# Turning one more head's output rows by transfers, between the steps of the last head's softmax

## The chip, the cores and the metric

The kernel runs on one core of one Trainium2 chip. The metric is the device time of one execution in microseconds (us). The kernel before was run three times: 1340.91, 1341.71 and 1341.49 us, median 1341.49 us.

## The reference

Two layers of a token backbone over 256 context tokens and 256 latent tokens of width 1024. Layer 0 mixes tokens with an mLSTM in two directions, layer 1 with multi-head attention; each is followed by a gated convolutional feed-forward, and a layer norm stands behind every sub-layer. The change lies in layer 0, between the last head's mixing and the output projection:

```python
def out(h_in, s):                                   # s: what the scan gives, per head
    o = jax.nn.sigmoid(h_in @ w_og).reshape(Bq, T, M_HEADS, M_DV)
    hsum = o * s.transpose(0, 2, 1, 3)              # the gate times the mixed values
    return _head_rms_norm(hsum, norm_g) @ w_out     # RMS norm per head, projection
```

There are four heads of 512 columns, 512 tokens (context first), and `w_out` is 2048 x 1024. The chunked scan is written in the kernel as one masked and normalised product per head, called its softmax here: exponentials of gate differences times the scores, a division, and the product with the values.

## The kernel before

Everything runs on one core and TensorE (PE) is busy throughout. A float32 product is made of three matmuls of rounded halves (`mm3`, lines 447, 450, 451): hi x hi, hi x lo, lo x hi. So every operand is written twice: a hi half, which ScalarE (ACT) casts, and a lo half, which VectorE (DVE) subtracts. Weights come through a stream: SyncE (SP) loads `raw` tiles, ACT casts them (line 361, `w` or `wu`), DVE subtracts (line 384).

The head loop in `build` goes over h = 0 to 3. In pass h the projection to queries and keys of head h (`w_qk`) fills PE, and background steps are taken between its weight tiles, by `tick`: the softmax of head h-1 (`head`), and the turn of the output rows of head h-2. Then `av` multiplies head h-1's softmax with its values, and `s_mm` makes head h's scores (tiles `sc`, `sl`, copied to `S` by ACT at line 1065).

*The softmax*, `head`: `aB` rows are loaded, DVE adds a mask (`Am`, line 1078), ACT takes exponentials (line 1115), DVE multiplies with the scores and sums (line 1116), divides (lines 1122 to 1133), and in a later step PE turns the result `W` in twelve 128x128 blocks (`PT`, line 1147), whose halves are cut at lines 461 and 462.

*The output rows*, `post`: `tt` are four tiles `oh` of 128 tokens x 512 columns, the product of `av` times the gate (DVE, line 1207). ACT squares and sums them (line 1217) and takes a root (line 1218), DVE inverts it (line 1219) and scales the rows (line 1221). The projection needs them turned (columns by tokens), as `hn`, four tiles for each head. There are two ways:

- By transfers, for heads 0 and 1: ACT copies the two 16-bit planes of each row tile apart (`pl`, line 466), the POOL queue writes them to DRAM (`hd`, line 1228), and ACT's queue loads them back turned (`hx`, line 1269, four transposes for each head). ACT and DVE make `hn` from `hx` (lines 1277 and 1278). `mixed` interleaves these steps with a softmax by a string of steps, in which `h` is a step of the softmax, `p` one of `post` (planes and writes), `L` a transpose and `S` the two halves of one `hn` tile.
- By PE, for heads 2 and 3: sixteen 128x128 turns into PSUM (`hnT`, line 1236), from which ACT and DVE make `hn` (lines 1243 and 1244).

After the loop comes the projection `mout`: sixteen weight tiles k, four for each head, 12 matmuls each for the first group of 256 tokens (`y`). Tiles 0 to 7 need heads 0 and 1. Between them run two background steps a tile: first all of head 3's softmax, then head 2's `post`. Also between them, head 3's values and gate rows are loaded (`v_steps`). Then `av(3)`, `post(3)` between tiles 8 to 11, and tiles 12 to 15. A scheduler then orders each engine's instructions; engines work in that order. Background work of another kind, sums for the layers' modulation (line 566, with its `ar` loads on SP and a one-element copy on ACT, line 581), is taken in between.

Of the kernel before, what the change touches and what calls it, by code (L numbers as in the profile page):

```python
# [416 lines left out]
class K:  # L417
# [827 lines left out]
            self.hn[k] = u  # L1245
        yield

    def mixed(self, head, post):

        plan = "p hp h hL h hL . L hS LS h S S . . ."  # L1250
        for step in plan.split():
            for op in step:
                if op in "hp":
                    next(head if op == "h" else post, None)
                elif op == "L":
                    self.turn_load()
                elif op == "S":
                    self.turn_split()
            yield
# [1106 lines left out]
def build(tc, off, a, out):  # L2366
    es = ExitStack()
    with es:
        k = K(tc, es, off, a)
# [14 lines left out]
        S = None  # L2384
        tt = None
        k.hn, k.turned, k.hx = {}, [], []
        for h in range(H0):
            gens = []
            if h == 0:
                gens.append(k.gate_chain())  # L2390
            if h >= 2:
                gens.append(k.mixed(k.head(h - 1, S), post))
            elif h >= 1:
                gens.append(k.head(h - 1, S))
            k.bg = gens
            k.w_qk(h, 2, (lambda: k.v_load(h - 1)) if h >= 1 else None)
            k.drain()
            if h >= 1:
                tt = k.av(h - 1)
                if h < 3:  # L2400
                    post = k.post(h - 1, tt)
                    next(post)
            S = k.s_mm(h)
        k.xc = None
        hn = lambda i: (k.hn[i][:, 0], k.hn[i][:, 1])
        pc = k.acc4()
        k.bg = [k.head(3, S, True), k.post(2, tt, True)]
        vs = k.v_steps(3)
        for i in range(8):
            k.outmm("mout", range(i, i + 1), hn, pc, 0, 16, 2)  # L2410
# [2 lines left out]
        tt = k.av(3)  # L2413
# [135 lines left out]
```

## Time and profile before

| | before |
|---|---|
| median of three runs | 1341.49 us |
| the profiled execution | 1341.12 us |
| its span in the profile | 1339.1 us |
| PE busy | 1326.7 us (99%) |
| DVE busy | 1077.2 us (80%) |
| ACT busy | 729.9 us (55%) |

Rows of a timeline give the start and the length in us, the engine, the line, the operation, the tiles and shapes, and, in brackets, how long the engine had been idle and what released it. Lengths overlap a little where an engine works without a pause, so the distance from one start to the next is what one instruction costs there. A row of waits names who waited for whom, the total, the times and the longest. Head 2's softmax and the way back of head 1 lie at 505 to 559 us of the span, head 3's softmax and the turn of head 2 at 571 to 598, `av(3)` at 598 to 606, and the turn of head 3 at 612.

### The profile page before, as it was taken

The page shows a single profiled execution, that of the slowest core. Times are in us where ns is not written, and L with a number is a line of the kernel's source. Part 1 is how long each engine was busy: PE and PEld are TensorE (multiplying, and loading weights), DVE is VectorE, ACT ScalarE, POOL GpSimd, SP SyncE. Part 2 cuts the span into 40 slices and gives each one's busy share as a digit, 9 for nine tenths or more (in the row PEclk, how much of TensorE's full clock was granted, in tenths as well). Part 3 has the DMA queues.
Part 4 walks back from the last instruction along what each step waited for, and adds up shares of the span by engine and source line. Part 5 has one row for each costly group of instructions (what it writes and reads, how often), then busy time and mean ns, then how long its engine had stood idle before and what let it go on. Part 6 is the DMA issues. An engine that isn't in the chain of part 4 may idle for free.

```text
span 1339.1 us, 18750 instructions
## 1 busy us (share of the span) xinstructions
PE 1326.7 (99%) x6573; PEld 1111.3 (83%) x6573; DVE 1077.2 (80%) x1783; ACT 729.9 (55%) x1271; POOL 165.3 (12%) x268
## 2 busy tenths in 40 slices
PE   8999999999999999999999999999999999999997
PEld 5777888888888888888898888888888988988876
DVE  4798957678688596987979978768899889899996
ACT  4765544445734555574643334333567768567772
POOL 0212000011110111120002011111000022020100
PEclk9999999999999999999999999999999999999999
DMA  9988947889685486875628989967967597497791
GB/s 366 324 276 290 333 161 252 243 270 313 235 262 190 156 245 200 295 276 209 228 75 276 322 264 283 280 177 180 321 223 221 175 243 222 165 303 233 250 336 49
DMA packets 116990, 325.52 MB, mean 243 GB/s; under 512 B 21416, under 2 KB 40360, under 8 KB 116624
## 3 DMA queue, kind: packets, MB, share of 16 engines
q1 hardware_dynamic: 64288, 223.37, 48.6%
q0 software_dynamic: 33360, 81.43, 22.7%
q10 hardware_dynamic: 19248, 19.54, 4.5%
q8 instruction: 51, 0.84, 0.2%
q14 instruction: 43, 0.35, 0.1%
HBM read 289.51 MB, written 56.80 MB: 259 GB/s over the span
## 4 chain that ended last, share of the span: by engine, by line
PE 98%; DVE 1%; DMA 0%; issue 0%; ACT 0%; SPq 0%; DVEq 0%; ACTq 0%
PE fin L1573 8%; PE y L450 6%; PE y L451 6%; PE y L447 6%; PE tok L447 6%; PE tok L450 6%; PE tok L451 6%; PE fin L447 6%; PE fin L451 6%; PE fin L450 6%; PE qk L447 4%; PE qk L451 4%; PE qk L450 4%; PE up L746 2%; PE up L447 2%; PE up L450 1%
## 5 line engine op out<-in xcount | busy, mean ns | idle before, releaser
L361 ACT CAST w<-raw 128x1024 fp32r<-128x1024 f32 (+2 forms) x290 | 300.0, 1037 | 263.6 <-PE tok L451 74.1
L384 DVE TENSOR_TENSOR w<-raw,w 128x1024 fp32r<-128x1024 f32 (+2 forms) x290 | 347.7, 1202 | 114.5 <-ACT w L361 111.0
L566 DVE SCALAR_TENSOR_TENSOR junk<-ar,bc 128x1024 f32<-128x1024 f32 x128 | 155.8, 1218 | 5.1 <-ACT bc L608 2.2
L450 PE MATMUL fin<-h,w 128*128 128x512 f32 (+1 forms) x370 | 139.6, 377 | 0.0
L447 PE MATMUL fin<-h,w 128*128 128x512 f32 (+1 forms) x370 | 139.5, 377 | 0.0
L451 PE MATMUL fin<-h,w 128*128 128x512 f32 (+1 forms) x370 | 139.3, 377 | 0.0
L1573 PE MATMUL fin<-h,w 128*128 128x512 f32 (+1 forms) x636 | 111.1, 337 | 0.0
L1573 PEld LDWEIGHTS fin<-h,w 128*128 128x128 f32 x636 | 97.6, 190 | 13.2
L447 PE MATMUL qk<-xc,w 128*128 128x512 f32 x256 | 100.1, 391 | 0.0
L451 PE MATMUL qk<-xc,w 128*128 128x512 f32 x256 | 99.7, 389 | 0.0
L450 PE MATMUL qk<-xc,w 128*128 128x512 f32 x256 | 99.6, 389 | 0.0
L450 PEld LDWEIGHTS fin<-h,w 128*128 128x128 f32 x370 | 69.6, 188 | 13.0
L451 PEld LDWEIGHTS fin<-h,w 128*128 128x128 f32 x370 | 69.6, 188 | 12.9
L447 PEld LDWEIGHTS fin<-h,w 128*128 128x128 f32 x370 | 69.6, 188 | 12.6
L451 PEld LDWEIGHTS qk<-xc,w 128*128 128x128 f32 x256 | 48.0, 188 | 10.0
L447 PEld LDWEIGHTS qk<-xc,w 128*128 128x128 f32 x256 | 48.1, 188 | 9.9
L450 PEld LDWEIGHTS qk<-xc,w 128*128 128x128 f32 x256 | 48.1, 188 | 9.9
L384 DVE TENSOR_TENSOR wu<-raw,wu 128x1024 fp32r<-128x1024 f32 (+1 forms) x42 | 49.6, 1205 | 4.7 <-ACT wu L361 4.3
L447 PE MATMUL tok<-w,hT 128*128 128x512 f32 x128 | 49.9, 390 | 0.0
L450 PE MATMUL tok<-w,hT 128*128 128x512 f32 x128 | 49.8, 389 | 0.0
L451 PE MATMUL tok<-w,hT 128*128 128x512 f32 x128 | 49.8, 389 | 0.0
L763 ACT ACTIVATE fg<-fg 128x512 f32<-128x512 f32 (+1 forms) x44 | 23.1, 525 | 47.6 <-DVE fg L761 41.2
(520 smaller groups left out, 3146.4 us busy)
## 6 DMA issues: line engine op xcount, KB each, us to landing
raw<-in_ws SPq DMA_DIRECT2D x279, 512.0 KB, 5.3
ar<-in_adaT SPq DMA_DIRECT2D x80, 512.0 KB, 5.7
t4d<-in_ws POOLq DMA_DIRECT2D x20, 512.0 KB, 8.6
zd<-in_ws POOLq DMA_DIRECT2D x18, 512.0 KB, 11.3
adaw<-in_ada SPq DMA_DIRECT2D x16, 512.0 KB, 7.9
raw<-zd SPq DMA_DIRECT2D x12, 512.0 KB, 5.2
zr<-fd ACTq DMA_DIRECT2D x33, 128.0 KB, 4.9
xmd<-xr POOLq DMA_DIRECT2D x16, 256.0 KB, 4.6
```

The source lines that it names most:

```text
L361: self.cast = k.nc.scalar.copy(h[:, :cols], src)
L384: i = self.k.nc.vector.tensor_sub(l[:, :n], src, h[:, :n])
L447: q = mm(out, w[0], x[0], start=start, stop=False, skip_group_check=on)
L450: mm(out, w[0], x[1], start=False, stop=False, skip_group_check=on)
L451: mm(out, w[1], x[0], start=False, stop=stop, skip_group_check=on)
L566: nc.vector.scalar_tensor_tensor(o, w, 1.0, self.bc[j], op0=ALU.mult, op1=ALU.mult, accum_out=col[:, k, j:j + 1])
L746: nc.tensor.matmul(ps[m], wk[i][:, c], hT[k][:, j], start=made[m] == 0, stop=made[m] == 23)
L763: nc.scalar.activation(tmp[:, :n], tmp[:, :n], AF.Silu)
L1573: self.nc.tensor.matmul(ps[:, 0:256] if x else ps, w[x][:, k * 128:(k + 1) * 128], h[:, 0:256] if x else h, start=i == 0 and not k0, stop= ...
```

## The change

Head 2's rows go by transfers too. `post` of head 2 is begun where head 2's product is made, ahead of head 3's scores, as for heads 0 and 1; so its squares, root and scaling stand there. `mixed` gets its string as an argument, and for the last softmax takes its ten steps first but for `post`'s planes and writes after the fourth, then the four transposes and the four pairs of halves:

```diff
-    def mixed(self, head, post):
-
-        plan = "p hp h hL h hL . L hS LS h S S . . ."
+    def mixed(self, head, post, plan="p hp h hL h hL . L hS LS h S S . . ."):
...
                 tt = k.av(h - 1)
-                if h < 3:
-                    post = k.post(h - 1, tt)
-                    next(post)
+                post = k.post(h - 1, tt)
+                next(post)
             S = k.s_mm(h)
...
-        k.bg = [k.head(3, S, True), k.post(2, tt, True)]
+        k.bg = [k.mixed(k.head(3, S, True), post, "h h h h p h h h h h h LL L L S S S S")]
```

Lines behind `mixed` move up by one. The built order changes on all engines between head 2's product and head 3's turn, and nowhere else. The string's `L` come behind `PT` there. Three places follow, first before, then after.

PE, the turns of head 3's softmax. `W` without a number is the tile of blocks 0 and 1 and that of block 3; `W_5091` and `W_5103` are the same tile, block 2:

```order
L447 MATMUL y<-wu,hn 128x512
L1147 MATMUL PT<-ident,W 128x128 x2
L1147 MATMUL PT<-ident,W_5091 128x128 x2
L1147 MATMUL PT<-ident,W 128x128 x2
L1147 MATMUL PT<-ident,W_5091 128x128 x2
L450 MATMUL y<-wu,hn 128x512
```

```order
L451 MATMUL y<-wu,hn 128x512
L1147 MATMUL PT<-ident,W 128x128 x6
L1147 MATMUL PT<-ident,W_5103 128x128 x2
L1147 MATMUL PT<-ident,W 128x128 x2
L1147 MATMUL PT<-ident,W_5103 128x128 x2
L447 MATMUL y<-wu,hn 128x512
```

Before, the four turns of blocks 0 and 1 stood 16 matmuls ahead of these eight, 24 behind the first `y<-wu`; now all twelve stand together, 36 behind it. The sixteen `hnT` of head 2, which stood 15 matmuls behind the eight, are gone.

ACT, from the last squares of head 2 (before) and the planes (after) to the next weight cast:

```order
L1217 ACTIVATE jk,ss<-oh 128x512 x2
L1218 ACT_TABLE_LOAD
L1218 ACTIVATE ss<-ss,keps 128x4
L461 CAST PT<-PT 128x512 x2
L1243 ACTIVATE hn<-hnT,sm 128x512 x4
L361 CAST w<-raw 128x1024
```

```order
L466 COPY pl<-oh 128x1024 x4
L461 CAST v<-vr 128x512
L361 CAST w<-raw 128x1024
L461 CAST v<-vr 128x512
L461 CAST PT<-PT 128x512 x3
L1268 DMA_TRANSPOSE hx<-hd 128x1024 x4
L1276 ACTIVATE hn<-hx,sm 128x512 x4
L361 CAST w<-raw 128x1024
```

The squares and the root of head 2, with a table load, now stand ahead of head 3's exponentials, which get a table load of their own; the root of head 3 gets a third.

DVE, from head 2's lo halves to the scaling of head 3's rows:

```order
L1244 SCALAR_TENSOR_TENSOR hn<-hnT,sm,hn 128x512 x4
L384 TENSOR_TENSOR w<-raw,w 128x1024
L1207 TENSOR_TENSOR oh<-av,oh 128x512 x2
L566 SCALAR_TENSOR_TENSOR junk,mod_84<-ar,bc 128x1024
L1207 TENSOR_TENSOR oh<-av,oh 128x512 x2
L1219 RECIPROCAL ss<-ss 128x4
L1221 TENSOR_SCALAR oh<-oh,ss 128x512 x4
```

```order
L1277 SCALAR_TENSOR_TENSOR hn<-hx,sm,hn 128x512 x4
L1207 TENSOR_TENSOR oh<-av,oh 128x512 x2
L384 TENSOR_TENSOR w<-raw,w 128x1024
L1207 TENSOR_TENSOR oh<-av,oh 128x512
L566 SCALAR_TENSOR_TENSOR junk,mod_84<-ar,bc 128x1024 x2
L1207 TENSOR_TENSOR oh<-av,oh 128x512
L1219 RECIPROCAL ss<-ss 128x4
L1221 TENSOR_SCALAR oh<-oh,ss 128x512 x4
```

The lo halves stand at the same place but read `hx`; one more sum (line 566) stands ahead of the last of head 3's products with the gate. Head 2's own inverse and scaling moved ahead of head 3's mask. On the POOL queue the four writes of `hd` stand ahead of the four gate loads `oh` of head 3.

## The prediction

> **What bounds the kernel now.** I read the page first, then who PE waited for, then the chain and the three engines' timelines around the change. The page's head, PE's row and the chain by engine:
>
> ```profile
> span 1339.1 us, 18750 instructions
> PE 1326.7 (99%) x6573; PEld 1111.3 (83%) x6573; DVE 1077.2 (80%) x1783; ACT 729.9 (55%) x1271; POOL 165.3 (12%) x268
> PE 98%; DVE 1%; DMA 0%; issue 0%; ACT 0%; SPq 0%; DVEq 0%; ACTq 0%
> ```
>
> PE is the bound from end to end. Its waits over the span (us in total, times, longest) are five rows, of which the largest and the smallest stand here; each came once, and none lies near the change:
>
> ```profile
> PE idle L683 <- DVE adav L519: 1.5, 1, 1.5
> ...
> PE up L746 <- DVE hT L721: 0.3, 1, 0.3
> ```
>
> So an instruction taken from PE is worth its whole time, if PE then finds everything else ready. The profiled execution took 1341.12 us, 2.0 us of it outside its span; the median is 1341.49. I add changes to the median: 0.4 us, within the spread of the three runs (1340.91 to 1341.71). About 0.2% (2.7 us) is what a measurement of this kernel can tell from no change.
>
> **What goes.** The chain in order of time, start and length, at the turns of head 2's softmax (543), of head 3's (587, 591) and of head 2's output rows (595):
>
> ```profile
> 543.40 1.31 PE PT L1147 x12
> ...
> 587.00 0.44 PE PT L1147 x4
> ...
> 591.11 0.87 PE PT L1147 x8
> ...
> 595.41 1.75 PE hnT L1236 x16
> ```
>
> The 16 turns of head 2 go: **1.75 us** off PE. The twelve PT turns stand in one piece after the change; that saves nothing, since 0.44 + 0.87 = 1.31, as head 2's twelve took. 1.75 us is 0.13%, so even the whole gain is inside what can't be told from none. hn's hi and lo halves are still made for head 2, by ACT and DVE, from hx instead of PSUM.
>
> **First place: does PE wait for the last softmax?** Before, by PE's order shown with the change, only the first four turns (blocks 0 and 1) stood 24 matmuls after the first `y<-wu`, the other eight 16 matmuls later. Now all twelve stand after 36; the fifth is the first that needs the last W. The rows of before that time this, PE and then DVE:
>
> ```profile
> 581.39 0.39 PE L447 MATMUL y<-wu,hn 128*128 128x512 f32 x1
> 598.16 0.39 PE L447 MATMUL av<-v,PT 128*128 128x512 f32 x1
> 606.32 0.39 PE L447 MATMUL y<-w,hn 128*128 128x512 f32 x1
> 611.77 1.91 PE L1236 MATMUL hnT<-ident,oh 128*128 128x128 f32 x16
> ```
>
> ```profile
> 571.32 0.68 DVE L1207 TENSOR_TENSOR oh<-av,oh 128x512 f32<-128x512 f32 x1
> 577.24 1.22 DVE L384 TENSOR_TENSOR w<-raw,w 128x1024 fp32r<-128x1024 f32 x1 [2.90 <-ACT w L361]
> 578.38 0.28 DVE L1116 SCALAR_TENSOR_TENSOR W<-W,S 128x128 f32<-128x128 f32 x1
> 584.42 0.67 DVE L462 TENSOR_TENSOR v<-vr,v 128x512 fp32r<-128x512 f32 x1
> 585.01 0.48 DVE L1131 TENSOR_SCALAR W<-W,R 128x512 f32<-128x512 f32 x1
> 590.01 0.75 DVE L1133 SCALAR_TENSOR_TENSOR W<-W,R 128x512 f32<-128x512 f32 x1
> ```
>
> 36 matmuls take 8.16 us (598.16 to 606.32), so PE reaches the turns at 581.39 + 8.16 = 589.55 and the fifth 0.44 later, at 590.0. DVE: L1219 and L1221 of head 2 (1.8 us) now stand ahead of the softmax of head 3, mostly in the 2.90 us in which DVE waited for ACT. ACT has head 2's root by about 574.9: the last L1207 ends at 572.0, then come a square (0.7), one S (0.6), the table load (1.3) and the root (0.3). Then DVE: 1.8 for L1219 and L1221, one Am (0.6), the `w` split (1.14), the other Am (0.6), to 579.1. Its rows from L1116 to the last L1133 took 578.38 to 590.76, 12.4 us. Behind that L1133 the order now has one `w` split (577.24 to 578.38, 1.14 us) and two `v` splits (584.42 to 585.01, 0.6 each) that stood ahead of it: 10.0 us remain. With 0.9 us of waiting for ACT's exponentials (next part; an estimate) W is ready at 579.1 + 10.0 + 0.9 = 590.0, as PE asks for it. I take 0.1 us of waiting, from 0 to 1.
>
> **What it adds on ACT.** ACT's rows; the first three are from the turn of head 0, whose rows go by transfers already, the rest from the place of the change:
>
> ```profile
> 459.50 3.88 ACT L466 COPY pl<-oh 128x1024 uint16<-128x1024 uint16 x4
> 465.74 1.28 ACT L1115 ACT_TABLE_LOAD   x1
> 467.10 0.40 ACT L1115 ACTIVATE W<-Am,gcol 128x128 f32<-128x128 f32 x1
> ...
> 571.00 0.59 ACT L1065 ACTIVATE S<-sc 128x512 f32<-128x512 f32 x1
> 577.11 0.69 ACT L1115 ACTIVATE W<-Am,gcol 128x128 f32<-128x128 f32 x2
> 582.28 0.60 ACT L461 CAST v<-vr 128x512 fp32r<-128x512 f32 x1
> 582.79 2.00 ACT L361 CAST w<-raw 128x1024 fp32r<-128x1024 f32 x2
> 589.46 1.28 ACT L1218 ACT_TABLE_LOAD   x1
> 590.75 0.30 ACT L1218 ACTIVATE ss<-ss,keps 128x4 f32<-128x4 f32 x1
> ```
>
> Before, one table load (589.46) served the roots of heads 2 and 3. Now head 2's root comes ahead of head 3's exponentials and head 3's behind, so there are three: root, exponential, root, two more. The Trainium skill, "ScalarE: Activation LUTs", section "What ACT_TABLE_LOAD costs", gives about 1283 ns for the load and 1380 ns of drain with it. The trace agrees on the first and shows no drain: 589.46 + 1.28 = 590.74 and L1218 runs at 590.75; with the drain each added load would cost 2.66.
>
> The four squares and head 2's root (about 4 x 0.7 + 1.6 us) fall in ACT's waits before 576 us. Then the second load (465.74 to 467.10: 1.36), one exponential and a late Am (0.5) delay the exponentials from 582.28 to 584.1. A `v` cast (0.5), a `w` cast (1.0) and the four pl copies (3.88) bring ACT to 589.5.
>
> **Second place: the way back.** hx and hd of heads 0 and 1 and the issues around them:
>
> ```profile
> L1269 ACTq DMA_TRANSPOSE hx<-hd x8: 1174/1208/1496, 471.7 to 534.4; - x8
> L1277 ACT ACTIVATE hn<-hx,sm x8: 722/727/746, 489.0 to 553.7; 128x512 fp32r<-128x512 f32 x8
> L1278 DVE SCALAR_TENSOR_TENSOR hn<-hx,sm,hn x8: 742/745/752, 493.0 to 558.9; 128x512 fp32r<-128x512 f32 x8
> DMA to landing us min/median/max: 3.4/3.6/4.4
> ...
> hd<-pl POOLq DMA_DIRECT2D x8, 256.0 KB, 3.1
> ```
>
> The last hd is issued at 589.5 and lands at 592.6; four transposes go out 1.21 apart, the last at 596.2. Their landing is 3.4 to 4.4 us; I take 4.1, since oh, xres and gate load beside them: 600.3. The last hi half (0.73) and lo half (0.75) end at 601.8. The projection asks for head 2's rows only at 606.32 - 1.65 = 604.7, so these halves themselves are on time. On POOL the `oh` loads of head 3 now stand behind hd:
>
> ```profile
> 584.35 1.26 POOL L1188 DMA_DIRECT2D oh<-od  x2 [9.85 <-PE y L450]
> ```
>
> They leave at about 590 instead of 584, some ten us before their use; no cost.
>
> But DVE works in order. By its rows shown with the change, head 3's four L1207 (its product times the gate, from which L1219 and L1221 make the norm that hnT waits for) now stand behind the four lo halves, which wait for a transfer, and a second L566 has slipped in ahead of the last. Their rows before:
>
> ```profile
> 601.78 1.22 DVE L566 SCALAR_TENSOR_TENSOR junk<-ar,bc 128x1024 f32<-128x1024 f32 x1
> ...
> 606.52 0.69 DVE L1207 TENSOR_TENSOR oh<-av,oh 128x512 f32<-128x512 f32 x1 [2.03 <-PE av L451]
> 608.39 0.18 DVE L1219 RECIPROCAL ss<-ss 128x4 f32<-128x4 f32 x1 [1.18 <-ACT ss L1218]
> 608.61 1.67 DVE L1221 TENSOR_SCALAR oh<-oh,ss 128x512 f32<-128x512 f32 x4
> ```
>
> From 601.8: three L1207 (0.6 each), a `w` split (1.1) and two L566 (2.4) put the last L1207 at 607.1. From it to the end of L1221 took 606.52 to 610.28, 3.8 us; the third table load now lies in that path: 607.1 + 3.8 + 1.3 = 612.2. PE can start 0.3 earlier (the third row block is turned first): 611.9. It arrives at 611.77 - 1.75 + 0.1 = 610.1, so it waits **1.8 us**. The same path without a late hx (av ends at 604.7) would end by 609.8: no wait. Ends: 0, and 5.1 if the transposes land as late as other loads do in this stretch (below).
>
> The same engine's later rows (two `w` splits, hnT's lo halves) shift with L1221 and keep about a microsecond before PE's use. SP's next `ar` load waits for the first L566, now some 12 us later; the weights queued behind it run six buffers ahead of their use, 2.7 us each (12 matmuls), so that costs nothing. Outside this stretch the two orders are the same.
>
> **Sum.** -1.75 + 0.1 + 1.8 = +0.15 us on 1341.49: about **1341.6 us**.
>
> **Rivals.**
> 1. *The whole gain.* Transfers are 2 us quicker than I take them, or ACT gets to the pl copies sooner. For: hx at its shortest (3.4) saves 0.7, and ACT's half microsecond waits are my estimates. Against: it needs all of them. 1341.49 - 1.75 = 1339.7.
> 2. *Slower: the transposes land late.* This stretch's xres loads, before the change:
>
> ```profile
> DMA to landing us min/median/max: 5.2/7.4/10.2
> 1.50 3.40 PE L683 MATMUL idle<-zero 128*128 128x512 f32 x8 [1.50 <-DVE adav L519]
> ```
>
> These loads now share the engines with the transposes. Were hx to land as slowly (7.4), 3.3 us more, hnT would wait 5.1: -1.75 + 0.1 + 5.1 = +3.5, 1344.9. An idle PE may also restart slowly: the first eight matmuls took 3.40 us where eight take 1.8 in the stretch above, 1.6 more, 1346.5. (The Trainium skill, "TensorE: Matmul & The Clock Gate", part 1, halves the clock after an idle window of about 3.4 us; no run here has shown so long a wait in mid-kernel.) Against: heads 0 and 1 landed within 4.4 with vr and oh loading beside them. It decides from a wait of 4.4 us at hnT, hx landing near 6.7.
> 3. *A table load holds ACT longer than its row.* Say it takes as long again (1.3), with work queued behind it. The load ahead of the exponentials then delays W and the pl copies by 1.3, and the one ahead of hnT adds 1.3: PE waits 1.4 at PT and 3.1 at hnT. -1.75 + 1.4 + 3.1 = +2.75: 1344.2. L1218's row, 0.01 us behind its load, speaks against it. By the drain that the Trainium skill gives (section above), 1.38 instead of 1.3, it would be 1344.4.
>
> **How the numbers follow.** Forecast (hnT waits 1 to 4 us, 1340.8 to 1343.8): 0.60. Whole gain or nearly (below 1340.8): 0.24. Late transposes: 0.10. Longer table loads: 0.03. Something outside this stretch that gains more than 2.7: 0.03. Range 1339.6 to 1344.4: the whole gain, up to the edge of rival 2. Faster by over 0.2%: 0.03; slower: 0.13; same: 0.84.
>
> **What would show it.** Right: 8 hx transposes become 12, three table loads from 570 to 610, no hnT of head 2 on the chain, and PE's waits gain one row, hnT waiting for DVE (oh L1221), of 1 to 3 us, perhaps PT waiting for W under 1. Wrong: no such row (rival 1), hnT's wait over 4 with hx landing over 6 (rival 2), or a wait of PE anywhere else, above all at the first `y` of head 2 or `av`.

## The result, and the profile after

The changed kernel takes **1363.89 us** (median of four runs, 1362.20 to 1367.88) against 1341.49: a ratio of 1.0176 (95% interval 1.0164 to 1.0188), 22.4 us slower. The profiled execution took 1364.58 us. The page's head and PE's row after the change:

```profile
span 1362.5 us, 18734 instructions
PE 1332.0 (98%) x6557; PEld 1113.2 (82%) x6557; DVE 1077.1 (79%) x1783; ACT 736.3 (54%) x1277; POOL 167.4 (12%) x272
```

Sixteen instructions are gone from PE, as planned, and yet PE is busy 5.3 us longer (1326.7 before). The waits of PE, largest first (total, times, longest):

```profile
PE y L447 <- ACT hn L1276: 10.0, 1, 10.0
PE hnT L1236 <- DVE oh L1221: 7.2, 1, 7.2
PE qk L451 <- DVE w L384: 1.5, 1, 1.5
...
PE PT L1147 <- DVE W L1133: 0.5, 1, 0.5
```

The first is new and was not in the sum: the projection waits for head 2's rows themselves. The second is the forecast one, four times as long. The third and `PT`'s lie at 538 to 546 us, in head 2's softmax, where PE's order is the same before and after; no other run's profile has the wait at `qk`. By windows, in which the columns are the stretch, its length, and busy time (and instructions) of PE, PEld, DVE, ACT and POOL, PE's granted clock, the DMA share and GB/s, the stretch 600 to 640 before and after:

```profile
600.00:640.00 40.00, 40.00 (x186) 33.38 (x185) 32.90 (x51) 19.23 (x33) 0.54 (x1) 1.00 0.54 200
```
```profile
600.00:640.00 40.00, 22.80 (x87) 18.41 (x87) 16.65 (x26) 13.85 (x25) 2.68 (x5) 0.74 0.83 184
```

In these 40 us PE ran 87 instructions instead of 186, at a mean clock of 0.74 of full speed: nearly all the loss is here. ACT's timeline leads to it:

```profile
594.24 1.18 ACTq L1268 DMA_TRANSPOSE hx<-hd  x1
594.32 0.58 ACT L461 CAST PT<-PT 128x512 fp32r<-128x512 f32 x1
595.45 20.66 ACTq L1268 DMA_TRANSPOSE hx<-hd  x3
616.22 1.34 ACT L1276 ACTIVATE hn<-hx,sm 128x512 fp32r<-128x512 f32 x2 [21.31 <-issue]
619.49 1.41 ACT L1276 ACTIVATE hn<-hx,sm 128x512 fp32r<-128x512 f32 x2 [1.94 <-DMA hx<-hd]
```

The first transpose is issued in 1.18 us, as before. The other three hold ACT's queue for 20.66 us, and for 21.31 us ACT does nothing: no cast, no half. The trace lists a landing for two of the four transposes (here and below, a landing time is the median of the two): the first landed 18.1 us behind its issue, at 612.4, and its half still waited for the fourth issue to end, at 616.1. The DMA view of 590 to 622 us lists what was in flight (issues, KB each, median us to landing):

```profile
xres<-in_tok POOLq DMA_DIRECT2D x8, 256.0 KB, 12.0
oh<-od POOLq DMA_DIRECT2D x4, 256.0 KB, 4.1
gate<-gd POOLq DMA_DIRECT2D x4, 256.0 KB, 8.2
...
hx<-hd ACTq DMA_TRANSPOSE x4, 19.5
```

Head 2's transposes took 19.5 us to land where heads 0 and 1 took 3.4 to 4.4 before, beside POOL loads of 256 KB: four `oh` and two `xres` issued up to 595.7, and eight more up to 608.4, while the transposes were in flight. The last two `gate` loads went out only at 618.

Behind the first wait the lo halves come at 616.97, and head 3's last product, the third table load and L1221 follow in DVE's order up to 632.0, which is the second wait. Each wait was followed by slow matmuls:

```profile
616.99 0.80 PE L447 MATMUL y<-w,hn 128*128 128x512 f32 x1 [9.98 <-ACT hn L1276]
617.58 0.63 PE L450 MATMUL y<-w,hn 128*128 128x512 f32 x1
618.01 0.63 PE L451 MATMUL y<-w,hn 128*128 128x512 f32 x1
...
620.90 0.39 PE L447 MATMUL y<-w,hn 128*128 128x512 f32 x1
621.13 0.40 PE L450 MATMUL y<-w,hn 128*128 128x512 f32 x1
...
631.70 3.68 PE L1236 MATMUL hnT<-ident,oh 128*128 128x128 f32 x16 [7.22 <-DVE oh L1221]
```

They start 0.43 us apart until 620.9 and 0.23 afterwards; nine took 3.9 us instead of 2.05. After the second wait the sixteen turns and six matmuls took 6.0 us instead of 3.1. **The account**: PE was 2.1 us late before it came to anything that the change touches, and 22.9 us late at the first `zT`, the turns behind this projection. Before, and after:

```profile
560.89 0.39 PE L447 MATMUL av<-v,PT 128*128 128x512 f32 x1
...
644.99 0.87 PE zT L1364 x8
```
```profile
563.03 0.39 PE L447 MATMUL av<-v,PT 128*128 128x512 f32 x1
...
667.91 0.87 PE zT L1363 x8
```

So 20.8 of the 23.4 us by which the span grew lie between these places. The two waits sum to 17.2, the slow matmuls to 1.9 + 2.9 = 4.8, the turns to -1.75: 20.25. The other half microsecond here, and as much behind `zT`, are not pinned to rows.

### The profile page after: what moved, and what is told of

It reads as the page before. It is cut to its first block, busy times and chain, and to the rows that moved or that the text cites. A ratio compares the mean times of both kernels' runs of the same rounds, so it can differ in the third digit from the quotient of the medians.

```text
span 1362.5 us, 18734 instructions
## 1 busy us (share of the span) xinstructions
PE 1332.0 (98%) x6557; PEld 1113.2 (82%) x6557; DVE 1077.1 (79%) x1783; ACT 736.3 (54%) x1277; POOL 167.4 (12%) x272
## 4 chain that ended last, share of the span: by engine, by line
PE 80%; issue 10%; DVE 3%; DMA 2%; ACT 2%; ACTq 1%; POOL 1%; SPq 0%; DVEq 0%; POOLq 0%
PE fin L1572 8%; PE tok L447 6%; PE tok L451 6%; PE tok L450 6%; PE fin L450 6%; PE fin L447 6%; PE fin L451 6%; PE y L450 5%; PE y L451 5%; PE y L447 5%; PE up L746 2%; PE up L447 1%; PE up L451 1%; PE up L450 1%; PE y L1415 1%
## 5 line engine op out<-in xcount | busy, mean ns | idle before, releaser
L566 DVE SCALAR_TENSOR_TENSOR junk<-ar,bc 128x1024 f32<-128x1024 f32 x128 | 155.8, 1217 | 6.2 <-ACT bc L608 3.2
```

Source lines behind the costliest of these rows:

```text
L566: nc.vector.scalar_tensor_tensor(o, w, 1.0, self.bc[j], op0=ALU.mult, op1=ALU.mult, accum_out=col[:, k, j:j + 1])
```

## The experiments

**Theory**: POOL's loads, in flight ahead of head 2's transposes and beside them, starve them; and since the transposes are instructions of ACT's queue, what stands behind them on ACT starves with them. **Rivals**: the norm or the table loads, moved ahead of head 3's softmax, cost it; or ACT's hold is its own; or the place is to blame (weights on SP's queue, four transposes in a row).

### xres and gate held back

```diff
+    def held_by(self, x):
+        if self.after is not None:
+            self.nc.vector.tensor_copy(x[0:1, 0:1], self.after)
...
             t = self.s2(name)
+            self.held_by(t)
...
                 x = self.s2("xres")
+                self.held_by(x)
...
+        k.after = k.hn[11][0:1, 1, 0:1].bitcast(F32)
```

> The change, with the twelve residual and gate loads (xres, gate) on the POOL queue held until the last lo half of head 2's hn is made, by a one-element copy into each tile. Theory A (the turned loads hx starve while loads of the POOL queue are in flight): hx lands within about 6 us of its issue, PE's 10.0 us wait for hn is gone and its wait at hnT falls from 7.2 to 1 to 3 us; 1340 to 1344 us. Theory B (hx is slow here by itself, for instance because hd is read right after it is written, or because four go out back to back): hx still lands after 15 us or more and the time stays above 1358 us.

Measured: 1347.89 us, ratio 1.0051 (1.0039 to 1.0064): two thirds of the loss are gone. Head 2's transposes land in 8.5 us, ACT's hold shrinks to 9.3 us, PE's wait at `y` is gone, the one at hnT is 6.3:

```profile
592.97 9.30 ACTq L1269 DMA_TRANSPOSE hx<-hd  x3
602.37 1.95 ACT L1277 ACTIVATE hn<-hx,sm 128x512 fp32r<-128x512 f32 x3 [9.94 <-issue]
```

Fewer loads, shorter hold: a dose, as the theory has it. But it missed the expected 1340 to 1344. The four `oh` loads still went out at 589.8 to 592.1, just ahead of the transposes.

### The norm and the table loads alone

```diff
-                if h < 3:
-                    post = k.post(h - 1, tt)
-                    next(post)
+                post = k.post(h - 1, tt, h == 3)
+                next(post)
...
-        k.bg = [k.head(3, S, True), k.post(2, tt, True)]
+        k.bg = [k.head(3, S, True), post]
```

> The kernel before, with head 2's squares, root and scaling moved ahead of head 3's scores as in the change, but its rows still turned by PE. It has the change's two added table loads and its early scaling, and no transfers. If the 22 us come from the transfers alone: 1341 to 1343 us. If the moved norm and the table loads carry a part of them: 1346 us or more.

Measured: 1340.90 us, ratio 1.0003 (0.9991 to 1.0014), and no new wait of PE. The first rival falls.

### The transposes issued, but not used

Head 2's rows go to PE again, and hx is loaded for nobody.

```diff
-            return
+            if h < 2:
+                return
...
-        k.bg = [k.mixed(k.head(3, S, True), post, "h h h h p h h h h h h LL L L S S S S")]
+        k.bg = [k.mixed(k.head(3, S, True), post, "h h h h p h h h h h h LL L L p . . .")]
```

> The change with its planes, writes and four transposes, but hn of head 2 made from PE's turn as before; nobody reads hx. Theory D (only the data of hx come late): PE waits for nothing new, 1341 to 1344 us. Theory Q (ACT's queue is held while it issues the transposes, and everything behind them on ACT is late): PE waits 8 us or more for ACT's hn or w halves, 1353 us or more.

Measured: 1358.63 us, ratio 1.0135 (1.0116 to 1.0153). Most of the loss stays though nothing waits for a transpose to land:

```profile
592.53 15.91 ACTq L1269 DMA_TRANSPOSE hx<-hd  x3
608.48 0.19 ACT L581 COPY mod<-w 1x1 f32<-1x1 f32 x1 [16.50 <-issue]
```
```profile
PE y L447 <- ACT hn L1244: 12.6, 1, 12.6
```

Behind the held issues stands ACT's whole work, here the hi halves from PE's turns. So the price has two parts, the late data and the held engine, and the second alone costs 18 us. They overlap and don't add: with ACT free, in the run on SP's queue below, the loss is as large as in the changed kernel.

### All of POOL's loads behind the transposes

```diff
+            nc.vector.tensor_copy(o[0:1, c.start:c.start + 1], self.lastx[0:1, 0:1])
             nc.gpsimd.dma_start(o[:, c], self.od[h, s])
...
         self.hx.append((h * 4 + e, x))
+        self.lastx = x
```

The four `oh` steps are also taken only after the first eight weight tiles.

> Edit: the four oh loads of head 3 wait, by a one-element copy on DVE, until the last hx transpose of head 2 has landed; xres and gate stand behind them on POOL's queue, so nothing of POOL's is in flight beside the transposes. On PE the sixteen hnT turns come one weight tile (12 matmuls, 2.7 us) later; the rest of the orders is the same. Theory (the POOL loads starve the transposes): hx of head 2 lands in 3.5 to 5 us, as at heads 0 and 1; the four issues are about 1.2 us apart and ACT's halves follow within 6 us of the last; no wait of PE at the first y of head 2; oh is issued near 601 and lands near 606, so PE may wait 0 to 3 us at hnT; 1340 to 1345 us. Rival (the place itself is the cause: the weight loads on SP's queue, or four transposes in a row): hx still lands in 7 us or more and ACT's issue stays held for 5 us or more, as with only xres and gate held; then oh comes later still and PE waits 5 to 10 us at hnT; 1347 to 1355 us.

Measured: 1348.43 us, ratio 1.0064 (1.0050 to 1.0078). The landing fell again, to 6.1 us, and ACT's three issues took 6.05. This is between the two expectations: longer than at heads 0 and 1 though nothing of POOL's is in the way, shorter than the rival's 7, with issues held as the rival had it (three free ones take 3.6). The hi halves run at 597.96 to 600.80 and the lo halves end at 601.6; the prediction had said 601.8. The time does not show it, because the edit makes a wait of its own:

```profile
607.50 0.69 DVE L1208 TENSOR_TENSOR oh<-av,oh 128x512 f32<-128x512 f32 x1 [1.40 <-DMA oh<-od]
609.83 0.69 DVE L1208 TENSOR_TENSOR oh<-av,oh 128x512 f32<-128x512 f32 x1 [1.64 <-DMA oh<-od]
611.32 0.69 DVE L1208 TENSOR_TENSOR oh<-av,oh 128x512 f32<-128x512 f32 x1 [0.80 <-DMA oh<-od]
```

`oh` is now late for head 3's products, and hnT waits 6.9 us.

### The transposes on SP's queue

```diff
-        self.nc.scalar.dma_start_transpose(x.bitcast(U16), d.rearrange("t h n -> (t h) n")[:, e * 128:(e + 1) * 128])
+        (self.nc.scalar if h < 2 else self.nc.sync).dma_start_transpose(x.bitcast(U16), d.rearrange("t h n -> (t h) n")[:, e * 128:(e + 1) * 128])
```

> Edit: the four transposes of head 2 are issued on SP's queue, among the weight loads, instead of ACT's; POOL's loads are as in the changed kernel. Theory (the transposes starve beside POOL's loads, and the queue that issues them is held): hx lands in 12 us or more, SP's row shows issues that take 5 us or more, ACT has no such hold; weights queued behind come late, so PE waits for hn of head 2 and perhaps for w: 1350 to 1375 us. Rival (the hold is ACT's own, by its casts and copies between the issues, and not the transfers'): hx lands in under 6 us and there is no wait at y: 1340 to 1346 us.

Measured: 1363.16 us, ratio 1.0156 (1.0138 to 1.0174). The hold moves with the issuing queue:

```profile
591.10 1.26 SPq L1268 DMA_TRANSPOSE hx<-hd  x1
592.46 0.52 SPq L324 DMA_DIRECT2D raw<-in_ws  x1
593.04 22.95 SPq L1268 DMA_TRANSPOSE hx<-hd  x3
```

The median landing is 18.1 us, about as from ACT's queue. ACT is free (its casts run on), and waits for the data instead; PE waits 11.3 us at `y` and 7.5 at hnT. The rival that the hold is ACT's own falls.

### The other way round: loads put beside head 1's transposes

This is the kernel *before*, with twelve transfers on POOL's queue that nobody reads.

```diff
...
+        if (h, e) == (1, 0):
+            src = self.a["tok"].rearrange("(t p) d -> t p d", p=128)
+            dm = self.dr.tile([12, 128, 512], F32, name="dm")
+            for i in range(12):
+                q = self.nc.gpsimd.dma_start(dm[i], src[i // 2 % 4][:, i % 2 * 512:i % 2 * 512 + 512])
+                self.behind(q, [self.lasta])
         x = self.s2("hx")
```

> Edit, on the kernel before: twelve transfers of 256 KB, memory to memory, that nobody reads are put on POOL's queue ahead of vr of head 2, so that they run as head 1's transposes are issued (530 to 535 us). Orders on the other engines are the same. Theory (POOL's transfers starve the transposes): hx of head 1, 3.4 to 4.4 us before, lands in 8 to 20 us, their issues take several us each, and ACT's exponentials behind them come late, so PE waits at PT: 1345 to 1370 us. Rival (only the place near the last softmax does it): head 1's hx still lands within 5 us with issues of 1.2 us; vr and oh come later but in time, 1341 to 1344 us.

Measured: 1365.47 us, ratio 1.0185 (1.0159 to 1.0211).

```profile
529.54 1.27 ACTq L1275 DMA_TRANSPOSE hx<-hd  x1
...
531.02 9.41 ACTq L1275 DMA_TRANSPOSE hx<-hd  x1
...
540.55 23.88 ACTq L1275 DMA_TRANSPOSE hx<-hd  x2
564.47 0.38 ACT L581 COPY mod<-w 1x1 f32<-1x1 f32 x3 [22.89 <-issue]
```
```profile
PE PT L1147 <- DVE W L1133: 26.2, 2, 23.2
```

Head 1's transposes, 4.1 us before, land in 33.0, and the kernel loses about as much as by the change. The twelve go from memory to memory, and `vr` and `oh` of head 2 came in behind them, so this crowd is another than head 2's. But the place near the last softmax is not needed: transfers on POOL's queue do it elsewhere too.

### Repairs

Four kernels try to give the transposes a free road without making `oh` late. In the first, POOL's queue takes `oh` ahead of `hd`, and a copy on DVE holds xres; one xres load still slips in ahead. The scheduler also moved one `pl` copy and two casts of `v` on ACT.

```diff
...
-                nc.gpsimd.dma_start(d[t * 128:(t + 1) * 128], pl)
+                q = nc.gpsimd.dma_start(d[t * 128:(t + 1) * 128], pl)
+                if h == 2:
+                    self.behind(q, [self.lasto])
...
                 x = self.s2("xres")
+                if self.lastx is not None:
+                    self.nc.vector.tensor_copy(x[0:1, 0:1], self.lastx[0:1, 0:1])
+                    self.lastx = None
```

> Edit: the changed kernel with POOL's queue in another order: oh of head 3 goes ahead of hd of head 2 (it then waits for its tiles until 584 and 587 us, as in the kernel before), and the first xres load waits, by a one-element copy on DVE, until the last transpose has landed and the first three products of head 3 are made, so xres and gate come behind. Only the end of the oh loads overlaps the first transposes. Theory (what is in flight on POOL's queue decides how long the transposes take): hx lands in 4 to 6.5 us as with all of POOL's loads behind them, with oh in time; no wait at the first y of head 2; hnT waits 0 to 3 us for head 3's norm; 1340 to 1343 us. If the oh loads still cost as much as with only xres and gate held, hx lands in 7 us or more, hnT waits about 6 us and it is 1347 to 1349 us.

Measured: 1344.46 us, ratio 1.0030 (1.0018 to 1.0042). The landing is 6.3 us, the wait at `y` is gone, hnT waits a little more than the 0 to 3 us expected, and starts slowly (3.13 us for sixteen turns, 1.91 before):

```profile
608.21 0.69 DVE L1205 TENSOR_TENSOR oh<-av,oh 128x512 f32<-128x512 f32 x1
611.36 0.18 DVE L1217 RECIPROCAL ss<-ss 128x4 f32<-128x4 f32 x1 [2.46 <-ACT ss L1216]
611.57 1.67 DVE L1219 TENSOR_SCALAR oh<-oh,ss 128x512 f32<-128x512 f32 x4
```
```profile
612.90 3.13 PE L1236 MATMUL hnT<-ident,oh 128*128 128x128 f32 x16 [3.51 <-DVE oh L1219]
```

In the second, the same with two of head 3's products between the lo halves:

```diff
-            nc.vector.tensor_tensor(self.oh[t], ts[t], self.oh[t], op=ALU.mult)
+            with self.tc.high_priority(400 if h == 3 else 0):
+                nc.vector.tensor_tensor(self.oh[t], ts[t], self.oh[t], op=ALU.mult)
```

> Edit: as the run before it, and the first two products of head 3 (L1207) stand on DVE between the lo halves of head 2 instead of behind them. Theory: the last product still stands behind two L566 (1.2 us each) and the third table load still lies in the path, so the wait at hnT changes by under 1 us; 1340 to 1343 us. If DVE's lo halves are what keeps head 3's norm, the wait is 1.5 us or more shorter than in the run before it.

Measured: 1345.54 us, ratio 1.0040 (1.0025 to 1.0055); hnT waits 3.0 us instead of 3.5, as expected; the time was not the 1340 to 1343 expected, and cannot be told from the run before it. The lo halves are not what keeps the norm.

In the third, from the first of these, the two L566 stand behind head 3's last product, and all of xres and gate behind the held one:

```diff
+                if self.prod is not None:
+                    self.behind(q, [self.prod])
...
+        if h == 3:
+            self.prod = q
```

> Edit: as the run with oh ahead of hd (its hnT wait 3.5 us), and the two L566 that stood ahead of head 3's last product on DVE now stand behind it; all xres and gate loads are behind the held one. Theory (hnT waits for the chain last product, third table load, L1219, L1221, as the sum had it): the last product comes 2.4 us sooner, the wait falls to about 1 us, PE's slow start goes with it, and the time comes down by 2 to 3.5 us, to 1341 to 1342.5 us. If the wait stays at 3 us or more, the chain is held by something else (oh or av of the last row block).

Measured: 1340.81 us, ratio 1.0003 (0.9990 to 1.0016), beside 1340.36 for the kernel before.

```profile
PE y L447 <- ACT u L1809: 1.1, 1, 1.1
PE hnT L1240 <- DVE oh L1223: 0.5, 1, 0.5
```

The transposes land in 5.8 us, hnT waits half a microsecond, and the whole 22 us are back. What the removed turns should save does not show.

In the fourth, head 3's turns also come one weight tile later:

```diff
+        yield
         g = self.smc("mng")
```

> Edit: as the run before it, and head 3's sixteen turns stand one weight tile (12 matmuls, 2.7 us) later on PE. Theory: no wait at hnT is left, so only the removed turns remain: 1339.2 to 1340.3 us, 1.75 us under the kernel before less at most some tenths (0.9987 of it). If it is 1341 us or more, something other than the waits at y and hnT costs what the turns save.

Measured: 1341.65 us, ratio 1.0008 (0.9998 to 1.0017): the gain of 1.75 us was expected and did not come. In its profiled execution (1342.93 us) the transposes landed in 9.8 us again, with POOL's queue held as in the run before. The DMA views of 588 to 606 us, of the third repair and of the fourth (packets, MB, share), differ in q1, SP's queue:

```profile
q10 hardware_dynamic: 4224, 1.05, 39.5%
q1 hardware_dynamic: 169, 0.63, 13.8%
```
```profile
q10 hardware_dynamic: 4224, 1.05, 49.3%
q1 hardware_dynamic: 288, 1.05, 22.8%
```

Weight loads moved 1.05 MB in this stretch, two whole ones, instead of 0.63, and hnT waited 1.7 us in spite of its later place. That the weight loads did it is argued from these rows; no run moved them alone. They are at most a part of it: from 599 to 601 us the fourth repair's transposes shared the engines with two packets of SP's queue and none of POOL's, and still moved only 0.06 MB. No version beat the kernel before.

## Why the prediction was wrong

It said 1341.6 us, at most 1344.4, and gave "slower" 0.13. Point by point:

- **The turns, -1.75**: PE lost its sixteen instructions; right as an entry, though no repaired kernel showed it in its time.
- **First place, PT, 0.1 (0 to 1)**: right. Head 3's turns ran at 591.69 and no wait is listed there; the 0.5 above is at head 2's turns, at 545.77.
- **Table loads, 1.3 each, no drain**: right. After the change the load ahead of the exponentials starts at 579.36, takes 1.28, and the next exponential runs at 580.66; and the norm and both loads moved alone cost nothing (1.0003).
- **Second place, "Their landing is 3.4 to 4.4 us; I take 4.1, since oh, xres and gate load beside them: 600.3"**: this step failed. Measured: 19.5 us, and the last pair at 619.5. Up to the first issue the working held (592.6 forecast; 594.24 measured, with PE 2.1 late). The landing was taken from heads 0 and 1, "with vr and oh loading beside them". For the most part these came behind. In the kernel before, from 532 to 536 us, while head 1's transposes ran, the DMA queues (packets, MB, share of 16 engines) were:

```profile
q10 hardware_dynamic: 3031, 0.75, 105.6%
q1 hardware_dynamic: 2, 0.00, 0.3%
```

q10, ACT's queue, had all engines, and POOL's queue (q0) not one packet; in the next two us q0 had 59 to q10's 997. The same view after the change, from 602 to 606 us:

```profile
q0 software_dynamic: 248, 0.82, 85.3%
q10 hardware_dynamic: 261, 0.07, 12.2%
```

In as many us the transposes got 0.07 MB, POOL's loads 0.82. Their packets are small (1.05 MB in 4224, about 250 bytes, against 3.3 KB for q0) and here the two queues moved about as many packets each. The Trainium skill, "DMA: Bandwidth & Descriptors", section "Queues, rings and completion order", says that a DMA engine goes round its queues packet by packet; by that, small packets lose in proportion to their size, if the packets of the trace are those of the page. The trace agrees in this stretch (261 to 248); in 606 to 610 us it was 844 to 210, so it is not the whole story.

- **The other half was not in the sum at all**: while the transfers of earlier transposes are slow, the next transpose's issue holds its queue. The prediction moved the four issues "1.21 apart" whatever happened, and asked only when the data would be there. With nothing waiting for the data the held queue alone cost 18 us.
- **Rival 2** named the right mechanism, transposes landing late, and priced it by xres's 7.4 us before the change. That row was of loads that were themselves part of the crowd, so no bound for what stands behind it: measured 19.5. Its slow restart (1.6 us) was right in kind: 1.9 and 2.9 us after waits of 10.0 and 7.2 us, with a granted clock of 0.52 (617.0 to 620.9) and 0.50 (631.7 to 637.7). Its reason against was the misread row above. Its "It decides from a wait of 4.4 us at hnT" looked at the wrong place, since `y` came to wait first, as the prediction's own list of what would show it wrong had it.
- **hnT, 1.8 us**: the chain was right. With the transposes at 6.3 us the last product began at 608.2 (the prediction had its end at 607.1), PE came 0.7 us earlier than said, and waited 3.5. The two L566 stood ahead of it from 605.72 to 608.21, the 2.4 us that the prediction gave them; in the third repair, with them behind the last product and the one xres load held too, the wait was 0.5.
- **POOL, "no cost"**: the `oh` loads of head 3 behind `hd` were judged by their own use alone. Their price was to the transposes; with xres and gate held they still made the landing 8.5 us, and ahead of `hd` 6.3.

What stays open: why the landing is 5.8 to 6.3 us and not 4 with POOL's loads out of the way, why the transposes can be slow with the engines nearly to themselves (fourth repair), and whether a gain is left in the third repair: its waits at hnT (0.5) and at `y` for `u` (1.1, 0.5 before) leave 0.65 of the 1.75 us, which its interval (-1.3 to +2.1 us) can't tell from nothing.

## What to carry to other kernels

A landing time in a trace belongs to what stood ahead of it on the other queues; before moving a transfer, look at the queues' packets in the old stretch and in the new one, and at what is issued just ahead there, not only at the GB/s. A transfer issued from a compute engine is work of that engine: if it may be slow, ask what stands behind its issue. And price a late transfer by a run with the crowd ahead of it, or leave the upper end wide open.

## What the runs showed of the hardware

- A transpose's issue on ACT took 1.2 us at the best, but three took 20.66 us beside POOL's loads, two took 23.88 with twelve extra transfers, and three 22.95 from SP's queue. The issue does not wait until an earlier transpose has landed: in the changed kernel the second ended at 607.34 us, the first landed at 612.4. By the packets of q10 in the DMA view (1056 for each transpose), 1063 to 1642 of those issued were still to come whenever one of the last three issues ended, in the changed kernel, with xres and gate held, and with the twelve transfers. So at the end of an issue never more than about one and a half transposes were still to come; that this bound is what holds the queue is argued, not shown.
- In one stretch 256 KB took 4.1 us as `oh`, issued ahead, and 19.5 as a transpose. Even alone the transposes, which take pieces of 256 bytes out of longer rows, moved 0.75 MB in 4 us, 188 GB/s; in the run with all of POOL's loads behind them, POOL's and SP's loads moved 386 GB/s from 608.4 to 617.2 us. The Trainium skill, "Advanced Engine Details and Errata", section "X-Bar Transpose (TRN2)", calls them as fast as regular DMAs and expects 350 to 400 GB/s; for these transposes the runs show about half of that.
- After waits of 10.0 and 7.2 us PE ran at about half speed (0.43 us a matmul instead of 0.23) for 3.9 and 6.0 us. The Trainium skill, "TensorE: Matmul & The Clock Gate", part 1, has it so for an idle window of about 3.4 us. Here a wait of 3.0 us was enough (second repair: sixteen turns took 3.59 us, 1.91 before), and one of 1.7 was not (fourth repair: 2.03).
